# Mixture-of-experts stage: experts ordered by place in group, result rows by expert number, first rows summed during the last experts

## The chip, the core and the metric

One core of one Trainium2 chip runs the program. The metric is device time in microseconds (us) of one execution; the kernel before takes 1620.63 us, the median of three runs.

## What is computed

One layer of a streaming encoder on 1024 tokens of width 1024, in float32: a normalised input, one combined projection, two kinds of attention (8 heads and 4 heads), gates and an output projection. Then comes the stage that the change touches: each token picks one of 4 groups and in it the best 2 of 8 experts, each a gated two-layer network of width 512.

```python
h = rms_norm(x, g_moe)
# group: argmax of h @ w_group; experts: the best 2 of the group's 8
yb = (silu(xb @ w1[e]) * (xb @ w3[e])) @ w2[e]      # for the tokens of expert e
x = x + sum over the token's two experts of weight * yb
out = rms_norm(x, g_final)
```

## The kernel before

**Routing.** While the output projection runs, `route_tile` (L735) finds for 128 tokens at a time the two experts `ix[0]` (higher score) and `ix[1]`, and writes a record into `rec`: token number (plus 1024 for the second choice) and weight. Matmuls with one-hot matrices spread the records into a table of 96 places by 32 experts. From it `slots` (L833) takes `gi` (which rows of the normalised input an expert gathers), `yi` (which row of the result buffer `ys` in DRAM each of its rows is scattered to: row t for the first choice of token t, row 1024 + t for the second) and `wt` (the weights).

**Experts.** `stage_moe` (L1050) goes through the 32 experts in turns e = 0 to 31, in the order of their numbers. PE's order is written out by hand, that of the other engines comes from a scheduler. In turn e PE runs: the 24 matmuls of w3 of this expert (`expert_up`, L971: per slice of 128 inputs one each with the high part, the low part and the high part again, L979 to L981); the 24 of w1 of the next expert, with the transposes of this expert's product `mg` (L998) before the last two slices; the transposes of a gathered input (L967); the 24 matmuls of w2 (`expert_down`, L1011 to L1013). After w3, DVE multiplies silu(w1 part) with the w3 part (`mg`, L990). The result `my` is scaled on ACT (L1018) and scattered to `ys` by POOL (L1022).

**Weights.** Each weight matrix comes in two loads of 1 MB (`expert_piece`, L930, 6 per expert), issued by SP one turn ahead into a ring of 11 slots (`mraw`), with at most three in flight. `expert_split` (L943) splits each into high and low parts: per load two copies on ACT (`mhi`, L45) and two subtractions on DVE (`mlo`, L46), 128x1024 each. A slot is free when its second subtraction is done.

**Tail.** In turn 31 `final_rows` (L1163) loads the rows of x that aren't in SBUF (tiles 0 to 3; 4 to 7 stay in `fx`) and `final_sums` (L1176) both result rows of every token, 1 MB for each of 8 tiles of 128 tokens; POOL adds the first row (L1184). The last expert's result isn't scattered: matmuls with a one-hot matrix `oh` add it in PSUM, together with the second row, which comes in through a matmul with the identity (L1109 to L1111). DVE adds the PSUM halves to x (L1112). `final_norm` (L1189) squares on ACT (L1192), takes the root on ACT (L1194) and the reciprocal on DVE (L1195), multiplies with the gains on DVE (L1196) and stores the tile (L1197).

```python
ps = self.pab.tile([128, 512], F32, name=f"m{n}", bufs=2 - n)
with self.tc.issue_after(self.last_down.ins):
    nc.tensor.matmul(ps, self.ident, Y[t][:, 1, nn], start=True, stop=False)
nc.tensor.matmul(ps, oh[:, t * 128:(t + 1) * 128], hl[0][:, nn], start=False, stop=False)
nc.tensor.matmul(ps, oh[:, t * 128:(t + 1) * 128], hl[1][:, nn], start=False, stop=True)
nc.vector.tensor_add(XS[t][:, nn], ps, XS[t][:, nn])
```

A branch (`overflow`, L1117) serves experts with over 96 tokens; it isn't entered here.

Of the kernel before, what the change touches and what calls it, by code (L numbers as in the profile page):

```python
# [32 lines left out]
CAP = 96  # L33
N_OVF = 21
# [17 lines left out]
class Block:  # L52
# [10 lines left out]
    def constants(self):  # L63
# [9 lines left out]
        self.eps = c.tile([128, 1], F32, name="eps")  # L73
        nc.vector.memset(self.eps, EPS)
# [626 lines left out]
    def route_setup(self):  # L701
# [20 lines left out]
        for k in range(2):  # L722
            nc.vector.tensor_scalar(self.rec[:, :, k, 0], self.tok2[:, :, k], -PAD_ID, None, op0=OP.add)
# [11 lines left out]
    def route_tile(self, t, lg):  # L735
# [194 lines left out]
    def expert_piece(self, e, i):  # L930
# [4 lines left out]
        src = self.a[("w1", "w3", "w2")[wi]][0, e].rearrange("(p c) n -> p c n", p=128)  # L935
# [66 lines left out]
    def expert_down(self, GT, w, wt, y=None, hl=None):  # L1002
        nc = self.nc
        if y is None:
            y = self.xp.tile([CAP, D], F32, name="my", bufs=1)
        ps = [self.py.tile([CAP, 512], F32, name="mpy") for _ in range(2)]
        for k in range(4):
            hi, lo = w[k // 2][k % 2]
            for n in range(2):
                nn = slice(n * 512, (n + 1) * 512)  # L1010
                nc.tensor.matmul(ps[n], GT[0][:, k], hi[:, nn], start=(k == 0), stop=False)  # L1011
                nc.tensor.matmul(ps[n], GT[0][:, k], lo[:, nn], start=False, stop=False)  # L1012
                self.last_down = nc.tensor.matmul(ps[n], GT[1][:, k], hi[:, nn], start=False, stop=(k == 3))  # L1013
        for n in range(2):
# [3 lines left out]
            nc.scalar.activation(y[:, nn], ps[n], AF.Copy, scale=wt)  # L1018
# [31 lines left out]
    def stage_moe(self, st):  # L1050
# [7 lines left out]
        gi, yi = self.gi, self.yi  # L1058
# [5 lines left out]
        for e in range(2):  # L1064
            self.expert_gather(X[e], gi[:, e:e + 1])
        XT = {e: self.expert_x(X[e]) for e in range(2)}
        self.expert_gather(X[0], gi[:, 2:3])
        up0 = self.expert_up(XT[0], weights(0, [0]))
        for e in range(N_EXP):
            last = e == N_EXP - 1  # L1070
            if e == 31:
                XS = self.final_rows(lambda: self.slot(True), self.fx)
# [4 lines left out]
            else:  # L1077
                Y = self.final_sums(self.slot, XS, False)

# [23 lines left out]

        for t in range(NT):
            for n in range(2):
                nn = slice(n * 512, (n + 1) * 512)
                ps = self.pab.tile([128, 512], F32, name=f"m{n}", bufs=2 - n)
                with self.tc.issue_after(self.last_down.ins):
# [4 lines left out]
            self.final_norm(t, XS[t], Y[t].rearrange("p k d -> p (k d)"))  # L1113
        self.yilast = self.rp.tile([CAP, 1], I32, name="yilast")
        nc.vector.tensor_copy(self.yilast, yi[:, N_EXP - 1:])

    def overflow(self):  # L1117
# [3 lines left out]
        with tc.If(n > 0):  # L1121
# [23 lines left out]
            with ExitStack() as st:  # L1145
# [3 lines left out]
                self.final_gains(self.pool(st, "opg", space=PSUM))  # L1149
                self.final_sums(y, X, True)  # L1150
                for t in range(NT):
                    self.final_norm(t, X[t], y())

    def final_gains(self, psum):

        g = self.gfin
        for n in range(2):
            ps = psum.tile([128, 512], F32, name=f"m{n}", bufs=2 - n)
            self.nc.tensor.matmul(ps, self.ones1[0:1, 0:1].to_broadcast([1, 128]), g[0:1, D + n * 512:D + (n + 1) * 512],
                                  start=True, stop=True)  # L1160
# [103 lines left out]
```

## Time and profile before

| | before |
|---|---|
| three runs | 1620.57, 1620.63, 1621.64 us |
| the profiled execution: time, span | 1615.66, 1613.8 us |
| mean granted clock of TensorE | 0.971 |
| PE busy | 1493.0 us (93%) |
| DVE, ACT, POOL busy | 1048.1, 882.5, 288.8 us |
| DMA, mean | 245 GB/s |

The span runs from the first to the last instruction of the profiled execution. Matmuls overlap their neighbours, so a PE that is busy all the time starts one every 0.23 us although each row shows 0.39. A bracket behind a row is the engine's idle time just before it and what ended it.

### The profile page before, as it was taken

The numbers are of one execution on the slowest core, as the hardware profiler recorded it, in microseconds if no ns is written. First come the engines' busy times: TensorE is split into PE (matmuls) and PEld (weight loads), VectorE is DVE, ScalarE is ACT, GpSimd is POOL, SyncE is SP. The second block draws the span as 40 slices with busy tenths as digits, with TensorE's granted clock in tenths as the row PEclk, the third lists the DMA queues.
The fourth block names the chain that finished last, engine by engine and source line by source line (L and its number), as shares of the span: only waits on it lengthen the run. The fifth ranks groups of instructions, "written<-read, shape, count | busy, mean of one in ns | idle before, by whom it ended". The sixth has DMA issues, their size and how long they took to land.

```text
span 1613.8 us, 21890 instructions
## 1 busy us (share of the span) xinstructions
PE 1493.0 (93%) x7713; PEld 1174.4 (73%) x7713; DVE 1048.1 (65%) x1926; ACT 882.5 (55%) x1327; POOL 288.8 (18%) x278
## 2 busy tenths in 40 slices
PE   6996999999999999996999959999999998999996
PEld 6994777777788888885888846666667666666663
DVE  6112555555555545545657459999999888888966
ACT  5212444444454444433312138878888877777764
POOL 2301122222221321210020131131011111111014
PEclk9998999999999999998999979999999999999998
DMA  8927566666644544349934759999999999999936
GB/s 267 332 96 236 139 179 171 164 161 162 159 134 129 166 151 131 111 148 248 313 112 144 313 202 337 377 354 368 385 376 375 374 344 356 346 350 342 351 133 253
DMA packets 181284, 394.94 MB, mean 245 GB/s; under 512 B 21714, under 2 KB 99538, under 8 KB 156594
## 3 DMA queue, kind: packets, MB, share of 16 engines
q1 hardware_dynamic: 174114, 376.89, 69.3%
q0 software_dynamic: 7056, 16.62, 3.1%
q8 instruction: 61, 1.00, 0.3%
q14 instruction: 53, 0.43, 0.1%
HBM read 324.36 MB, written 77.25 MB: 249 GB/s over the span
## 4 chain that ended last, share of the span: by engine, by line
PE 79%; DVE 8%; DMA 6%; issue 4%; ACT 2%; SPq 1%; POOL 1%; ACTq 0%; DVEq 0%; POOLq 0%
PE pz L305 7%; PE pz L306 7%; PE pz L307 7%; PE m L980 6%; PE m L981 6%; PE m L979 6%; PE mpy L1013 3%; PE mpy L1011 3%; PE mpy L1012 3%; DVE mlo L46 3%; PE po L472 2%; PE pt L386 2%; PE ps L360 2%; PE ps L361 2%; DMA mraw<-in_w_dram 2%
## 5 line engine op out<-in xcount | busy, mean ns | idle before, releaser
L46 DVE TENSOR_TENSOR mlo<-mraw,mhi 128x1024 fp32r<-128x1024 f32 x384 | 450.1, 1219 | 40.5 <-ACT mhi L45 38.7
L45 ACT ACTIVATE mhi<-mraw 128x1024 fp32r<-128x1024 f32 x384 | 391.7, 1056 | 64.3 <-PE m L981 46.6
L980 PE MATMUL m<-mlo,XT 128*96 128x512 f32 x512 | 205.6, 402 | 22.3 <-DVE mlo L46 22.3
L305 PE MATMUL pz<-ht,zhi 128*128 128x512 f32 x512 | 215.6, 421 | 0.0
L979 PE MATMUL m<-mhi,XT 128*96 128x512 f32 x512 | 206.5, 403 | 0.0
L981 PE MATMUL m<-mhi,XT 128*96 128x512 f32 x512 | 205.1, 401 | 0.0
L307 PE MATMUL pz<-ht,zlo 128*128 128x512 f32 x512 | 202.5, 396 | 0.0
L306 PE MATMUL pz<-ht,zhi 128*128 128x512 f32 x512 | 201.3, 393 | 0.0
L369 ACT ACTIVATE te<-te,nm 128x256 f32<-128x256 f32 (+7 forms) x128 | 99.2, 775 | 145.1 <-DVE nm L365 145.1
L980 PEld LDWEIGHTS m<-mlo,XT 128*96 128x96 f32 x512 | 84.3, 165 | 64.8 <-DVE mlo L46 31.0
L365 DVE CUSTOM_DVE_ANT_0 te<-ps,nF 128x512 f32<-128x512 f32 (+3 forms) x128 | 75.0, 588 | 76.8 <-PE ps L361 48.6
L46 DVE TENSOR_TENSOR PT<-pt,PT 128x512 fp32r<-128x512 f32 (+1 forms) x144 | 77.0, 554 | 73.3 <-ACT PT L45 71.4
L277 POOL TENSOR_TENSOR zlo<-zraw,zhi 128x1024 fp32r<-128x1024 f32 x32 | 76.7, 2398 | 209.9 <-ACT zhi L276 208.9
L307 PEld LDWEIGHTS pz<-ht,zlo 128*128 128x128 f32 x512 | 96.7, 189 | 21.9
L45 ACT ACTIVATE PT<-pt 128x512 fp32r<-128x512 f32 (+1 forms) x144 | 66.4, 488 | 84.2 <-PE pt L386 57.6
L981 PEld LDWEIGHTS m<-mhi,XT 128*96 128x96 f32 x512 | 84.1, 164 | 35.4 <-issue 0.5
L979 PEld LDWEIGHTS m<-mhi,XT 128*96 128x96 f32 x512 | 84.3, 165 | 34.4 <-issue 0.6
L305 PEld LDWEIGHTS pz<-ht,zhi 128*128 128x128 f32 x512 | 98.4, 192 | 13.5
L306 PEld LDWEIGHTS pz<-ht,zhi 128*128 128x128 f32 x512 | 97.7, 191 | 13.6
L1013 PE MATMUL mpy<-mhi,GT 128*96 128x512 f32 x256 | 101.7, 397 | 2.8 <-DVE GT L46 2.5
L1011 PE MATMUL mpy<-mhi,GT 128*96 128x512 f32 x256 | 102.3, 400 | 0.6 <-ACT GT L45 0.6
L1012 PE MATMUL mpy<-mlo,GT 128*96 128x512 f32 x256 | 100.4, 392 | 0.0
(263 smaller groups left out, 2797.1 us busy)
## 6 DMA issues: line engine op xcount, KB each, us to landing
mraw<-in_w_dram SPq DMA_DIRECT2D x192, 1024.0 KB, 8.1
zraw<-in_w_in_dram SPq DMA_DIRECT2D x32, 512.0 KB, 4.3
ys<-zero SPq DMA_DIRECT2D x16, 512.0 KB, 4.9
gscr<-sh SPq DMA_DIRECT2D x32, 256.0 KB, 2.0
o<-oscr SPq DMA_DIRECT2D x8, 1024.0 KB, 7.5
g<-gscr SPq DMA_DIRECT2D x32, 256.0 KB, 4.5
mraw<-ys SPq DMA_DIRECT2D x8, 1024.0 KB, 10.9
xt<-in_x_dram SPq DMA_DIRECT2D x8, 512.0 KB, 5.0
```

Of the source, the lines that this page charges most:

```text
L45: nc.scalar.activation(hi, src, AF.Copy)
L46: nc.vector.tensor_tensor(lo, src, f32(hi), op=OP.subtract)
L305: nc.tensor.matmul(ps, hi[:, k], self.hT[0][:, k, tk], start=(k == 0), stop=False)
L306: nc.tensor.matmul(ps, hi[:, k], self.hT[1][:, k, tk], start=False, stop=False)
L307: nc.tensor.matmul(ps, lo[:, k], self.hT[0][:, k, tk], start=False, stop=(k == KC - 1))
L369: nc.scalar.activation(t[:, :n], t[:, :n], AF.Exp, scale=-1.0, bias=nm, accum_out=rs)
L979: nc.tensor.matmul(ps, XT[0][:, k], hi, start=(k == 0), stop=False)
L980: nc.tensor.matmul(ps, XT[0][:, k], lo, start=False, stop=False)
L981: nc.tensor.matmul(ps, XT[1][:, k], hi, start=False, stop=(k == KC - 1))
L1011: nc.tensor.matmul(ps[n], GT[0][:, k], hi[:, nn], start=(k == 0), stop=False)
L1012: nc.tensor.matmul(ps[n], GT[0][:, k], lo[:, nn], start=False, stop=False)
L1013: self.last_down = nc.tensor.matmul(ps[n], GT[1][:, k], hi[:, nn], start=False, stop=(k == 3))
```

## The change

- `ORDER` puts the experts in the order 0, 8, 16, 24, 1, 9, ... 7, 15, 23, 31: first each group's first expert, last each group's last.
- In `route_tile` the two records of a token are numbered by expert number: the smaller of its two experts gets row t, the larger row 1024 + t. The last four turns (28 to 31) serve each group's last expert, which is never the smaller one, so rows 0 to 1023 are whole after turn 27's scatter.
- `final_rows` moves from turn 31 to turn 28, with its three slots (they don't go back to the ring), and loads the gains broadcast to 128 partitions. `final_add` replaces `final_sums`: turns 29 and 30 load and add the first rows of four tiles each, turn 31 loads the second rows; all sums are on DVE. The matmuls with the identity, those that spread the gains, and POOL's sums go.
- `final_norm` takes the root by a power on POOL; odd tiles are scaled by one instruction on DVE, even tiles by a copy on ACT and a product on POOL.

```diff
+ORDER = [g * PER_GRP + l for l in range(PER_GRP) for g in range(N_GRP)]
...
-        for k in range(2):
-            nc.vector.tensor_scalar(self.rec[:, :, k, 0], self.tok2[:, :, k], -PAD_ID, None, op0=OP.add)
+        nc.vector.tensor_scalar(self.tok2, self.tok2, -PAD_ID, None, op0=OP.add)
...
+        sw = p.tile([128, 1], F32, name="sw")
+        nc.vector.tensor_scalar(sw, ix[0], ix[1], float(S), op0=OP.is_lt, op1=OP.mult)
+        nc.vector.tensor_add(self.rec[:, t, 0, 0:1], self.tok2[:, t, 0:1], sw)
+        nc.vector.tensor_sub(self.rec[:, t, 1, 0:1], self.tok2[:, t, 1:2], sw)
...
-            if e == 31:
-                XS = self.final_rows(lambda: self.slot(True), self.fx)
...
-            else:
-                Y = self.final_sums(self.slot, XS, False)
+            if e == N_EXP - 4:
+                XS = self.final_rows(lambda: self.slot(True), self.fx)
+            if N_EXP - 4 < e < N_EXP - 1:
+                h = e - N_EXP + 3
+                self.final_add(self.slot, XS, 0, range(4 * h, 4 * h + 4))
+            if last:
+                Y = self.final_add(self.slot, XS, 1, range(NT))
...
+        junk = self.slot(True)
...
-                ps = self.pab.tile([128, 512], F32, name=f"m{n}", bufs=2 - n)
-                with self.tc.issue_after(self.last_down.ins):
-                    nc.tensor.matmul(ps, self.ident, Y[t][:, 1, nn], start=True, stop=False)
-                nc.tensor.matmul(ps, oh[:, t * 128:(t + 1) * 128], hl[0][:, nn], start=False, stop=False)
-                nc.tensor.matmul(ps, oh[:, t * 128:(t + 1) * 128], hl[1][:, nn], start=False, stop=True)
+                ps = self.pab.tile([128, 512], F32, name="m0", bufs=2)
+                for i in range(2):
+                    nc.tensor.matmul(ps, oh[:, t * 128:(t + 1) * 128], hl[i][:, nn], start=(i == 0), stop=(i == 1))
                 nc.vector.tensor_add(XS[t][:, nn], ps, XS[t][:, nn])
...
+    def final_add(self, tile, X, k, ts):
+
+        nc = self.nc
+        Y = {}
+        for t in ts[::2]:
+            y = tile()
+            nc.sync.dma_start(y.rearrange("p (t d) -> p t d", t=2), self.ys[k * S + t * 128:k * S + (t + 2) * 128].rearrange("(t p) d -> p t d", p=128))
+            for i in range(2):
+                Y[t + i] = y[:, i * D:(i + 1) * D]
+                nc.vector.tensor_add(X[t + i], X[t + i], Y[t + i])
+        return Y
...
+        ss = self.fp.tile([128, 1], F32, name=f"ssf{t % 2}")
+        nc.scalar.activation(junk, x, AF.Square, accum_out=ss)
+        r = self.rstd(self.fp, ss, D, f"rf{t % 2}")
+        if t % 2:
+            nc.vector.scalar_tensor_tensor(y, x, r, self.gfin, op0=OP.mult, op1=OP.mult)
+        else:
+            nc.scalar.activation(x, x, AF.Copy, scale=r)
+            nc.gpsimd.tensor_tensor(y, x, self.gfin, op=OP.mult)
+        self.nc.sync.dma_start(self.a["out"][0, t * 128:(t + 1) * 128], y)
```

**DVE between the products of turns 29 and 30**, before. `mg` is the product of a turn (the first here is turn 30's), `mlo` a subtraction of weights; 14789 is the last load of expert 30's w2, 14949 the first of the next expert's w1.

```order
L46 TENSOR_TENSOR mlo<-mraw_14787,mhi 128x1024 x2
L46 TENSOR_TENSOR mlo<-mraw_14789,mhi 128x1024 x2
L46 TENSOR_TENSOR mlo<-mraw_14949,mhi 128x1024
L990 TENSOR_TENSOR mg<-m_14977,mg 96x128x4
L46 TENSOR_TENSOR mlo<-mraw_14949,mhi 128x1024
```

The same place with the change (14826 is the last load of w2, 14994 the first of the next w1; 14649 and 14652 hold x of tiles 0 to 3, 14828 and 14832 their first rows):

```order
L48 TENSOR_TENSOR mlo<-mraw_14824,mhi 128x1024 x2
L48 TENSOR_TENSOR mlo<-mraw_14826,mhi 128x1024 x2
L1187 TENSOR_TENSOR mraw_14649<-mraw_14649,mraw_14828 128x1024 x2
L994 TENSOR_TENSOR mg<-m_15030,mg 96x128x4
L1187 TENSOR_TENSOR mraw_14652<-mraw_14652,mraw_14832 128x1024 x2
L48 TENSOR_TENSOR mlo<-mraw_14994,mhi 128x1024 x2
L48 TENSOR_TENSOR mlo<-mraw_14996,mhi 128x1024 x2
```

Four sums stand ahead of the first subtraction of the last expert's w1, where before one subtraction stood ahead of the product.

**DVE from the last splits to the tail**, with the change (`GT` is the low part of the transposed product of turn 31, X_9655 and the `mlo` beside it the parts of the last expert's result; L1119 is the sum from PSUM, L1112 before):

```order
L48 TENSOR_TENSOR mlo<-mraw_15004,mhi 128x1024 x2
L1187 TENSOR_TENSOR fx_8979<-fx_8979,mraw_15006 128x1024
L994 TENSOR_TENSOR mg<-m_15196,mg 96x128x4
L1187 TENSOR_TENSOR fx_8981<-fx_8981,mraw_15010 128x1024
L48 TENSOR_TENSOR GT_15241<-mpt,GT_15240 128x384
L51 SCALAR_TENSOR_TENSOR mlo<-mpy,sw,X_9655 96x512
L1187 TENSOR_TENSOR mraw_14649<-mraw_14649,mraw_15156 128x1024 x2
L1187 TENSOR_TENSOR mraw_14652<-mraw_14652,mraw_15160 128x1024 x2
L1119 TENSOR_TENSOR mraw_14649<-m_15281,mraw_14649 128x512
L1187 TENSOR_TENSOR fx_8979<-fx_8979,mraw_15164 128x1024
```

Each `fx` sum shown has a second one behind it. Before, nothing stood between the last splits, `mg` and `GT`, and the tail on DVE began with the sums from PSUM.

**SP**, with the change, from turn 28's loads on (14645 is the last load of expert 29, 14647 the gains, 14994 the first load of the last expert):

```order
L940 DMA mraw_14645<-in_w_dram 128x2048
L1169 DMA mraw_14647<-in_g_final_dram 128x1024
L1175 DMA mraw_14649<-x_7590 128x1024 x2
L940 DMA mraw_14816<-in_w_dram 128x2048
L940 DMA mraw_14826<-in_w_dram 128x2048
L1184 DMA mraw_14828<-ys 128x2x1024
L1184 DMA mraw_14832<-ys 128x2x1024
L940 DMA mraw_14994<-in_w_dram 128x2048
L1184 DMA mraw_15006<-ys 128x2x1024
L1184 DMA mraw_15156<-ys 128x2x1024
```

Of the weight loads only the first and last of an expert are shown. The loads of x and of the first rows now stand between the weight loads; before, all stood behind the last one.

## Rows read from the trace of the kernel before

**Rows 1.** Busy time in stretches of the end: start and end, length, busy us and instructions of PE, PEld, DVE, ACT and POOL, granted clock of TensorE, DMA share, GB/s.

```profile
1503.00:1523.00 20.00, 19.31 (x92) 13.49 (x91) 17.97 (x22) 16.54 (x21) 2.10 (x2) 1.00 0.94 355
1543.00:1562.00 19.00, 18.31 (x82) 12.63 (x81) 15.72 (x15) 14.56 (x18) 1.05 (x1) 1.00 0.17 63
1600.00:1614.00 14.00, 3.90 (x12) 1.75 (x10) 6.92 (x11) 3.50 (x9) 0.00 (x0) 0.80 0.38 152
```

**Rows 2.** The timeline (start, duration) of POOL's last four scatters, the issue of the last weight load and of the first result load by SP, and the same stretch's DMA times to landing (last two rows).

```profile
1521.97 1.45 POOL L1022 DMA_INDIRECT ys<-my,sy  x1 [17.53 <-ACT my L1018]
1543.47 1.05 POOL L1022 DMA_INDIRECT ys<-my,sy  x1 [20.05 <-ACT my L1018]
1562.24 1.20 POOL L1022 DMA_INDIRECT ys<-my,sy  x1 [17.72 <-ACT my L1018]
...
1529.91 0.33 SPq L936 DMA_DIRECT2D mraw<-in_w_dram  x1
1565.92 0.37 SPq L1183 DMA_DIRECT2D mraw<-ys  x1
...
mraw<-in_w_dram SPq DMA_DIRECT2D x13, 1024.0 KB, 5.7
ys<-my,sy POOLq DMA_INDIRECT x2, 7.1
```

**Rows 3.** The timeline of DVE around the products of turns 29 and 30.

```profile
1527.53 3.49 DVE L46 TENSOR_TENSOR mlo<-mraw,mhi 128x1024 fp32r<-128x1024 f32 x3
...
1544.17 3.50 DVE L46 TENSOR_TENSOR mlo<-mraw,mhi 128x1024 fp32r<-128x1024 f32 x3 [0.45 <-ACT mhi L45]
1548.08 1.10 DVE L990 TENSOR_TENSOR mg<-m,mg 96x512 f32<-96x512 f32 x1 [0.41 <-PE m L981]
1549.09 4.62 DVE L46 TENSOR_TENSOR mlo<-mraw,mhi 128x1024 fp32r<-128x1024 f32 x4
```

**Rows 4.** PE at the start of w1's matmuls in turn 30, then in turn 29.

```profile
1547.88 0.40 PE L979 MATMUL m<-mhi,XT 128*96 128x512 f32 x1
1548.11 0.39 PE L980 MATMUL m<-mlo,XT 128*96 128x512 f32 x1
1550.35 0.47 PE L980 MATMUL m<-mlo,XT 128*96 128x512 f32 x1 [0.69 <-DVE mlo L46]
...
1528.80 0.47 PE L980 MATMUL m<-mlo,XT 128*96 128x512 f32 x1 [2.03 <-DVE mlo L46]
```

**Rows 5.** Busy time in stretches, columns as in rows 1.

```profile
1530.00:1533.00 3.00, 3.00 (x9) 1.95 (x8) 3.00 (x3) 1.06 (x1) 0.00 (x0) 0.50 0.84 306
1566.00:1568.20 2.20, 0.55 (x4) 0.37 (x4) 1.02 (x1) 0.49 (x1) 0.00 (x0) 1.00 0.48 110
1568.20:1574.00 5.80, 5.78 (x24) 3.71 (x24) 0.56 (x1) 0.54 (x1) 2.87 (x2) 1.00 1.03 421
1585.00:1588.50 3.50, 0.48 (x3) 0.05 (x1) 3.50 (x4) 0.00 (x0) 3.50 (x2) 0.90 1.03 405
1588.50:1594.00 5.50, 5.49 (x9) 3.06 (x10) 2.60 (x4) 2.89 (x6) 3.88 (x2) 0.50 0.39 156
```

**Rows 6.** The timeline of turn 31 on DVE and PE, from the last splits to the last expert's down matmuls.

```profile
1562.94 2.36 DVE L46 TENSOR_TENSOR mlo<-mraw,mhi 128x1024 fp32r<-128x1024 f32 x2 [0.29 <-ACT mhi L45]
1566.02 1.02 DVE L990 TENSOR_TENSOR mg<-m,mg 96x512 f32<-96x512 f32 x1 [0.71 <-PE m L981]
1568.20 0.56 DVE L46 TENSOR_TENSOR GT<-mpt,GT 128x384 fp32r<-128x384 f32 x1 [1.17 <-ACT GT L45]
...
1568.81 0.47 PE L1013 MATMUL mpy<-mhi,GT 128*96 128x512 f32 x1
1573.72 0.40 PE L1013 MATMUL mpy<-mhi,GT 128*96 128x512 f32 x1
```

**Rows 7.** The timeline of the tail: POOL's last sums, the splits of the last expert's result on DVE, two products with the gains on DVE and a sum from PSUM beside POOL's sums, the last product and the last store.

```profile
1581.10 2.37 POOL L1184 TENSOR_TENSOR fx<-fx,mraw 128x1024 f32<-128x1024 f32 x1 [0.19 <-DMA mraw<-ys]
1583.66 8.72 POOL L1184 TENSOR_TENSOR fx<-fx,mraw 128x1024 f32<-128x1024 f32 x3 [0.19 <-DMA mraw<-ys]
...
1574.17 1.45 DVE L49 SCALAR_TENSOR_TENSOR mlo<-mpy,sw,X 96x512 fp32r<-96x512 f32 x2 [5.41 <-ACT X L48]
1582.67 1.89 DVE L1196 SCALAR_TENSOR_TENSOR mraw<-mraw,rfr,mraw 128x1024 f32<-128x1024 f32 x1
1585.14 2.71 DVE L1196 SCALAR_TENSOR_TENSOR mraw<-mraw,rfr,mraw 128x1024 f32<-128x1024 f32 x1
1587.78 0.68 DVE L1112 TENSOR_TENSOR mraw<-m,mraw 128x512 f32<-128x512 f32 x1
1607.02 1.28 DVE L1196 SCALAR_TENSOR_TENSOR mraw<-fx,rfr,mraw 128x1024 f32<-128x1024 f32 x1
1608.34 0.33 SPq L1197 DMA_DIRECT2D out_dram<-mraw  x1
```

**Rows 8.** Durations by line: instructions, count, ns least/median/most, first and last start.

```profile
L125 DVE TENSOR_SCALAR r2m<-ss x8: 153/154/155, 801.0 to 944.7; 128x1 f32<-128x1 f32 x8
L127 POOL TENSOR_TENSOR r1r<-r1m,mhalf x8: 548/550/1583, 6.4 to 36.9; 128x1 f32<-128x1 f32 x8
L1192 ACT ACTIVATE mraw<-fx x4: 1057/1058/1059, 1596.5 to 1605.3; 128x1024 f32<-128x1024 f32 x4
L1192 ACT ACTIVATION_READ_ACCUMULATOR mraw<-fx x4: 185/186/188, 1597.5 to 1606.3; 128x1 f32 x4
```

More of the change, by code (lines that the diff above doesn't have):

```diff
@@ L1012, in expert_down @@
                 nc.tensor.matmul(ps[n], GT[0][:, k], lo[:, nn], start=False, stop=False)
-                self.last_down = nc.tensor.matmul(ps[n], GT[1][:, k], hi[:, nn], start=False, stop=(k == 3))
+                nc.tensor.matmul(ps[n], GT[1][:, k], hi[:, nn], start=False, stop=(k == 3))
         for n in range(2):
@@ L1057, in stage_moe @@
         self.moe_pools(st, True)
-        gi, yi = self.gi, self.yi
+        gi, yi, wt = [[x[:, o:o + 1] for o in ORDER] for x in (self.gi, self.yi, self.wt)]
         def weights(e, ms):
@@ L1148, in overflow @@
                 X = self.final_rows(y, {})
-                self.final_gains(self.pool(st, "opg", space=PSUM))
-                self.final_sums(y, X, True)
+                self.fp = p
+                for k in range(2):
+                    self.final_add(y, X, k, range(NT))
                 for t in range(NT):
[L1152 to L1160, printed above, removed]
-            self.nc.scalar.activation(g[:, n * 512:(n + 1) * 512], ps, AF.Copy)
+                    o = y()
+                    self.final_norm(t, X[t], o[:, :D], o[:, D:])
     def final_rows(self, tile, X):
         nc = self.nc
-        g = self.gfin = tile()
-        nc.sync.dma_start(g[0:1, D:], self.a["g_final"].rearrange("(o d) -> o d", o=1))
+        self.gfin = tile()[:, :D]
+        nc.sync.dma_start(self.gfin, self.bcast(self.a["g_final"]))
         ts = [t for t in range(NT) if t not in X]
@@ L1174, in final_rows, with final_norm @@
         return X
-    def final_sums(self, tile, X, both):
+    def final_add(self, tile, X, k, ts):
         nc = self.nc
-        Y = []
-        for t in range(NT):
-            y = tile().rearrange("p (k d) -> p k d", k=2)
-            Y.append(y)
-            nc.sync.dma_start(y, self.ys.rearrange("(k t) d -> t k d", k=2)[t * 128:(t + 1) * 128])
-            nc.gpsimd.tensor_tensor(X[t], X[t], y[:, 0], op=OP.add)
-            if both:
-                nc.vector.tensor_add(X[t], X[t], y[:, 1])
+        Y = {}
[5 more added lines that the diff above has]
+                nc.vector.tensor_add(X[t + i], X[t + i], Y[t + i])
         return Y
-    def final_norm(self, t, x, y):
+    def final_norm(self, t, x, junk, y):
         nc = self.nc
-        ss = self.rp.tile([128, 1], F32, name="ssf", bufs=2)
-        nc.scalar.activation(y[:, :D], x, AF.Square, accum_out=ss)
-        r = self.rp.tile([128, 1], F32, name="rfr", bufs=2)
-        nc.scalar.activation(r, ss, AF.Sqrt, scale=1.0 / D, bias=self.eps)
-        nc.vector.reciprocal(r, r)
-        nc.vector.scalar_tensor_tensor(y[:, D:], x, r, self.gfin[:, :D], op0=OP.mult, op1=OP.mult)
-        nc.sync.dma_start(self.a["out"][0, t * 128:(t + 1) * 128], y[:, D:])
+        ss = self.fp.tile([128, 1], F32, name=f"ssf{t % 2}")
[3 more added lines that the diff above has]
+            nc.vector.scalar_tensor_tensor(y, x, r, self.gfin, op0=OP.mult, op1=OP.mult)
+        else:
+            nc.scalar.activation(x, x, AF.Copy, scale=r)
+            nc.gpsimd.tensor_tensor(y, x, self.gfin, op=OP.mult)
+        self.nc.sync.dma_start(self.a["out"][0, t * 128:(t + 1) * 128], y)
     def run(self):
```

31 lines of the change are left out of this document (15 added, 16 removed).

## Prediction

> **What bounds the kernel now.** I read the busy time by stretches first. In the experts' stage PE works 19.31 of 20 us and DVE 17.97, in turns 30 and 31 still 18.31 and 15.72 of 19 [rows 1]: PE sets the pace, DVE has some 2 us to spare in a turn, and DMA falls to a share of 0.17 once the last weights are in. In the last 14 us PE is busy 3.90 and nothing runs through. So I look at two things apart: when the last expert's down matmuls end (last start 1573.72 [rows 6], end about 1574.1; I call it T), and how long the tail is from T to the end.
>
> Next come the waits at the joints of the turns. PE starts w1's matmuls at 1547.88 and stops at 1550.35 for a subtraction on DVE [rows 4]; that one began at 1549.09, behind the product at 1548.08 [rows 3]. DVE's place in its list at the joint, not its load over a turn, is what PE feels. In the tail, DVE's last product starts at 1607.02, 34.2 us after T it ends (1608.30), and from there to the end of the span are 5.5 us for store and closing [rows 7]. The tail is 39.7 us.
>
> All terms below are against this profiled execution: 1615.66 us, span 1613.8. The median of the runs is 1620.63; I add the sum to the median. A measurement of this kernel tells about 0.2%, 3.2 us, from no change.
>
> **Routing: +0.4.** Three small DVE instructions more per tile, 153 ns each by the nearest row [rows 8]. Seven of the eight tiles have them beside the output projection's matmuls; without that cover they would cost 0.45 each. The last tile's stand in DVE's list ahead of the records that the first gather waits for: 0.4 (0 to 0.45). The order of the experts itself, the eps constant and the gathers cost nothing: as many rows and bytes move, in another order.
>
> **Loads: 0.** The same 8 MB of result rows are read, 4 MB of them earlier; new are 0.5 MB for the gains. Three of 11 slots leave the ring at turn 28. A weight load goes out as the slot 11 loads back is free: the last one went at 1529.91 [rows 2], when the second of the splits begun at 1527.53 ended [rows 3]. With 8 slots the last expert's loads go when the same-numbered loads of the expert before are split: the first at 1529.9, the last at 1546.5. They are split from about 1546.5 (first) to 1562.94 (last) [rows 3, 6] and land 5.7 us after issue [rows 2]: 10 us to spare. The first-row loads wait on SP for turn 28's scatter, 1521.97 + 7.1 = 1529.1 [rows 2], and the last expert's weights queue behind them, but those had no slot before 1529.9. The scatter of turn 29 now waits on POOL for these loads; they land by about 1537, it goes at 1543.47. Nothing is late; if landings took 10 us more, a rival below.
>
> **Four sums ahead of the last expert's first split: +4.4.** A sum reads two SBUF tiles of 128x1024 like a subtraction of weights: 3.50/3 to 4.62/4 = 1.16 us in a row [rows 3]. DVE ends w2's last split at 1546.5 (1544.17 and two of three). Then, by the list: two sums to 1548.8, the product (1.0) to 1549.8, two sums to 1552.1, the first split to 1553.3. PE has been ready for it since 1548.11 [rows 4]. Before, PE's eighth matmul ran at 1550.35, which is a start without a stop at 1550.35 - 7 x 0.231 = 1548.73; now the second runs at 1553.35, a start at 1553.12. Difference 4.4. The splits after it come every 1.16 us, six matmuls take 1.39, so no second wait. Lower bound 3.3 (if the first pair of sums were done in DVE's gaps), upper 5.
>
> **The clock after that stop: +2.7.** After the stop of 2.03 us in turn 29 [rows 4] the granted clock is 0.50, the 1.2 GHz level, for 3 us and somewhat more; nine matmuls run in a stretch that holds 13 at full clock [rows 5], which with its edges cost 1.65. After 3.02 idle us of PE in the tail the clock is 0.50 for 5.5 us [rows 5]: 2.75 lost. The new stop is over 5 us, nearest to the second: 2.7 (1.6 to 2.75).
>
> **Four sums in turn 31: +2.7.** The last split ends at 1565.30 [rows 6]; two sums take DVE to 1567.6, so the product starts 1.6 later than 1566.02. Two sums follow it, 2.3, ahead of the low part of GT: it starts at 1570.9 in place of 1568.20, and PE's third down matmul needs it. 2.7 (2 to 3). All this on top of the shift already there.
>
> **The clock after that: +1.6.** Before, PE was idle 1.7 us in two pieces here and kept its clock of 1.00 [rows 5]. Now the first piece alone is 2.5 us; the nearest row is the 2.03 of turn 29, priced 1.65. Bounds 0 and 2.75.
>
> **The tail: +3.0.** Off PE go the 32 identity matmuls and the gains; off POOL eight sums of 2.37; off ACT the roots and a table load. On DVE come eight sums of 1.16 and 8 factors of 0.15 in place of reciprocals; four products of 1.28 leave for ACT (1.06) and POOL (2.37 each, as its sums [rows 7]). POOL gets eight powers of 0.55 [rows 8]. DVE's own work is then 8 x 1.16 + 16 x 0.67 + 4 x 1.28 + 2 x 0.73 + 8 x 0.15 = 27.8 us. What matters is who waits for whom in the lists, so I go through them with these durations, 0.07 us per handover.
>
> A product on DVE beside POOL's sums takes 1.89 and 2.71 in place of 1.28, POOL's three sums 8.72 in place of 7.1, while the sum from PSUM keeps 0.68 [rows 7]. So I let instructions that read two SBUF tiles on both engines exclude each other. This way the list of before gives T to the last product 33.9, against 34.2 in the trace; without exclusion it gives 30.4. The new list gives: first split of the result 0.9, two sums 3.3, second split and two sums 6.5, tile 0's halves 7.8, two sums 10.2, tile 1's first half 11.1, a sum 12.3, then DVE waits for POOL's first product until 14.7; the last half of tile 7 ends at 31.3, its square 32.6, factor and power 33.5, its product 34.8; tile 6 has its copy on ACT behind tile 7's square and its product on POOL until 37.2. So 37.2 against 34.2: +3.0. Bounds: 33.9 without exclusion (-0.3), 38.2 if the matmuls run at the lower clock (+4).
>
> The Trainium skill ("SBUF — State Buffer", section Who interferes with whom) says that a VectorE instruction with two SBUF inputs and a GpSimd instruction that reads SBUF hold a shared port for the whole instruction, and that one with a single SBUF input stays free of it. Rows 7 agree for sums and products. For the powers on POOL, 128x1, no run here shows whether they are held up as well in the tail; by the rule they are, and the tail is the 37.2 above, otherwise about 0.5 less.
>
> **Sum.** 0.4 + 4.4 + 2.7 + 2.7 + 1.6 + 3.0 = 14.8, so 1620.6 + 14.8 = 1635.4; I say 1635.
>
> **Rivals.**
> - **DVE waits, no clock, no exclusion.** The joints cost 4.4 + 2.7, the clock nothing (as at 1566 to 1574 [rows 5]) and the tail -0.3: 7.2 with the routing, 1628. For it: the clock's fall isn't the same after each stop. Chance 0.17.
> - **Faster: the sums are free on DVE.** POOL pays 2.37 for a sum, DVE 1.16; if DVE reached the sums of turns 29 and 30 in its 2 us of spare time per turn [rows 1], T would stay, and the tail would be DVE's own 27.8 plus the last copy and product, about 31 against 34.2: 3.2 less, with the routing 1618; with an earlier end of the last square, 1615. It decides if the joints cost under the tail's gain. Against it: DVE's list is kept in order, and at 1544 to 1549 it has 0.45 and 0.41 of idle time [rows 3]. The Trainium skill ("GPSIMD Engine Reference", section 4.1 Engine selection) puts elementwise sums on VectorE, about twice as fast; the prices agree, and by that rule the tail would gain. Chance 0.10.
> - **Weights late.** If the scatter of turn 28 lands 10 us later than 7.1, SP holds the last expert's loads until about 1540 and its splits come at 1548 to 1551: that is still ahead of the sums' end; only beyond does each us count. With 6 us more: 1641. Chance 0.05.
> - **No change.** Joints of 3 to 5 us, and a tail shorter by as much: 1620. Chance 0.06. That the change doesn't move the sums is excluded by the lists.
>
> **How the numbers follow.** Forecast 0.62, for 1635, own range 1630 to 1640. The range 1625 to 1641 takes in the first rival and the bounds of the terms (low 0 + 3.3 + 0 + 2 + 0 - 0.3 = 5; high 0.45 + 5 + 2.75 + 3 + 2.75 + 4 = 18, of which not all are likely at once); it leaves out the two other cases and the late weights. Slower by over 0.2%: 0.62 + 0.17 + 0.05 = 0.84; within: 0.06; faster: 0.10.
>
> **What would show it.** In the profile after: PE idle some 5 us in front of the last expert's second w1 matmul, ended by DVE's subtraction, and behind it a stretch at clock 0.50; an idle time of over 2 us before GT's transposes and a wait for GT's low part; L1187 rows of about 1.16; T about 12 us later, near 1586; then 37 us to POOL's last product. It is wrong if DVE's sums start earlier than w2's last split, if T moves by less than 4 us, or if the tail after T is shorter than 34 us.

## Result and the profile after

Four runs of the changed kernel take 1629.96 to 1634.97 us, median 1630.44; four of the kernel before beside them 1621.11. The ratio is 1.0064 (95% 1.0045 to 1.0082): slower, by 7 to 13 us. The forecast was 1635, its range 1625 to 1641.

The profiled execution took 1629.96, its span is 1628.1, against 1615.66 and 1613.8 before. Of the 14.3 us between the spans 13.4 lie in the last three stretches of this table. I cut at marks that both traces have: POOL's scatters of turns 29 and 30, and DVE's first split of the last expert's result (`mlo` <- `mpy`), which starts at the end of the last down matmul.

| | before | changed | difference |
|---|---|---|---|
| start to the scatter of turn 29 | 1543.47 | 1544.37 | +0.9 |
| from there to the scatter of turn 30 | 18.77 | 23.90 | +5.1 |
| from there to the first split of the result | 11.93 | 16.49 | +4.6 |
| from there to the end | 39.63 | 43.34 | +3.7 |

DVE of the changed kernel, in order of time (start, duration, line, tiles, count, idle time ahead). L48 are the splits, L1187 the sums, L994 `mg`; [rows 3, 6] hold this piece of before:

```profile
1545.07 2.36 DVE L48 TENSOR_TENSOR mlo<-mraw,mhi 128x1024 fp32r<-128x1024 f32 x2 [0.48 <-ACT mhi L47]
1547.35 2.35 DVE L1187 TENSOR_TENSOR mraw<-mraw,mraw 128x1024 f32<-128x1024 f32 x2
1549.62 1.02 DVE L994 TENSOR_TENSOR mg<-m,mg 96x512 f32<-96x512 f32 x1
1550.56 2.35 DVE L1187 TENSOR_TENSOR mraw<-mraw,mraw 128x1024 f32<-128x1024 f32 x2
1552.83 4.62 DVE L48 TENSOR_TENSOR mlo<-mraw,mhi 128x1024 fp32r<-128x1024 f32 x4
...
1571.26 2.35 DVE L1187 TENSOR_TENSOR fx<-fx,mraw 128x1024 f32<-128x1024 f32 x2
1573.53 1.01 DVE L994 TENSOR_TENSOR mg<-m,mg 96x512 f32<-96x512 f32 x1
1574.45 2.35 DVE L1187 TENSOR_TENSOR fx<-fx,mraw 128x1024 f32<-128x1024 f32 x2
1576.72 0.55 DVE L48 TENSOR_TENSOR GT<-mpt,GT 128x384 fp32r<-128x384 f32 x1
1584.76 0.75 DVE L51 SCALAR_TENSOR_TENSOR mlo<-mpy,sw,X 96x512 fp32r<-96x512 f32 x1 [7.49 <-ACT X L50]
```

No sum has idle time ahead of it: DVE goes without a pause from the splits through the sums to `mg` and on to the last expert's first split. The same view of PE shows three places where DVE kept it idle; the bracket says how long and what ended it. [rows 4] have the first place before. The line behind the `...` is before's wait at the second. At the third PE did not wait for DVE before:

```profile
1554.09 0.74 PE L984 MATMUL m<-mlo,XT 128*96 128x512 f32 x1 [4.92 <-DVE mlo L48]
1574.59 0.56 PE L1002 MATMUL mpt<-ident,mg 96*128 96x96 f32 x4 [1.76 <-DVE mg L994]
1577.32 0.74 PE L1016 MATMUL mpy<-mhi,GT 128*96 128x512 f32 x1 [0.43 <-DVE GT L48]
...
1567.09 0.55 PE L998 MATMUL mpt<-ident,mg 96*128 96x96 f32 x4 [1.11 <-DVE mg L990]
```

PE's 0.69 us ahead of the second w1 matmul has become 4.92. The stretches behind it (length, then busy time and count of PE, PEld, DVE, ACT, POOL, then the granted clock, DMA share and GB/s):

```profile
1548.70:1554.00 5.30, 0.47 (x2) 0.00 (x1) 5.30 (x6) 1.19 (x2) 0.00 (x0) 0.73 0.96 359
1554.00:1560.40 6.40, 6.31 (x22) 4.37 (x23) 5.31 (x6) 2.13 (x3) 0.00 (x0) 0.69 0.78 302
1578.00:1584.90 6.90, 6.83 (x23) 4.32 (x21) 0.14 (x1) 0.84 (x2) 0.00 (x0) 0.72 0.80 330
1600.00:1628.10 28.10, 9.52 (x18) 4.43 (x18) 11.93 (x20) 9.76 (x15) 13.40 (x11) 0.50 0.38 151
```

After each stop part of the next 6 to 7 us runs at the lower level (granted clock 0.69 and 0.72 over these stretches), and the end of the tail, where PE is busy for 9.52 of 28.1 us, stays at it (0.50). POOL in the tail (L127 the power, L1200 the product of an even tile):

```profile
1594.32 3.22 POOL L127 TENSOR_TENSOR rf0r<-rf0m,mhalf 128x1 f32<-128x1 f32 x1 [25.14 <-DVE rf0m L125]
...
1616.81 3.28 POOL L1200 TENSOR_TENSOR mraw<-fx,mraw 128x1024 f32<-128x1024 f32 x1 [0.23 <-ACTq L1130]
```

POOL's last product ends at 1620.09, 35.3 us behind the first split, and the span goes on for 8.0 us, where before 5.5 followed DVE's last product [rows 7]. At the end of its list POOL runs a drain of 5.2 us. The changed kernel, then before (count, ns least/median/most, first and last start):

```profile
L1264 POOLq DRAIN  x3: 46/107/5213, 1622.0 to 1627.8; - x3
L1260 POOLq DRAIN  x3: 46/107/5213, 1594.3 to 1613.5; - x3
```

The long one is the first. Before it started at 1594.3, beside other work; now it starts at 1622.0, behind the last product.

### The profile page after: what moved, and what is told of

It is laid out like the page before. It is cut to its first block, busy times and chain, and to the rows that moved or that the text cites. A ratio compares the mean times of both kernels' runs of the same rounds, so it can differ in the third digit from the quotient of the medians.

```text
span 1628.1 us, 21837 instructions
## 1 busy us (share of the span) xinstructions
PE 1491.4 (92%) x7677; PEld 1171.6 (72%) x7677; DVE 1060.3 (65%) x1960; ACT 882.9 (54%) x1320; POOL 286.4 (18%) x282
## 5 line engine op out<-in xcount | busy, mean ns | idle before, releaser
L48 DVE TENSOR_TENSOR mlo<-mraw,mhi 128x1024 fp32r<-128x1024 f32 x384 | 450.1, 1220 | 43.1 <-ACT mhi L47 41.6
L984 PEld LDWEIGHTS m<-mlo,XT 128*96 128x96 f32 x512 | 84.8, 166 | 69.4 <-DVE mlo L48 35.3
L48 DVE TENSOR_TENSOR PT<-pt,PT 128x512 fp32r<-128x512 f32 (+1 forms) x144 | 77.0, 554 | 72.6 <-ACT PT L47 70.6
L305 PEld LDWEIGHTS pz<-ht,zhi 128*128 128x128 f32 x512 | 98.5, 192 | 14.4 <-ACT zhi L276 0.5
```

The source lines that it names most:

```text
L48: nc.vector.tensor_tensor(lo, src, f32(hi), op=OP.subtract)
L305: nc.tensor.matmul(ps, hi[:, k], self.hT[0][:, k, tk], start=(k == 0), stop=False)
L984: nc.tensor.matmul(ps, XT[0][:, k], lo, start=False, stop=False)
```

## Experiments

The table has the median, the ratio to the kernel before on the same chip, and the last two stretches as above: joints (scatter of turn 29 to first split of the result) and tail (from there to the end). The kernel before has other medians beside other runs: 1621.1 beside the changed kernel, 1617.5 beside e2 to e4, 1618.9 beside e5 to e8, 1620.0 beside e9 and e10. So kernels are compared by their ratios, not by their times.

| | us | ratio (95%) | joints | tail |
|---|---|---|---|---|
| before, first profile | | | 30.7 | 39.6 |
| e1 before again | 1617.61 | | 32.3 | 40.5 |
| changed | 1630.44 | 1.0064 (1.0045 to 1.0082) | 40.4 | 43.3 |
| e2 sums one column | 1622.37 | 1.0033 (1.0020 to 1.0045) | 33.7 | 43.3 |
| e3 sums placed | 1621.67 | 1.0024 (1.0015 to 1.0034) | 33.8 | 41.4 |
| e4 products on DVE | 1627.41 | 1.0056 (1.0041 to 1.0071) | 39.6 | 40.6 |
| e5 split before mg | 1619.02 | 1.0003 (0.9991 to 1.0015) | 32.3 | 41.4 |
| e6 norm without POOL | 1624.26 | 1.0045 (1.0031 to 1.0059) | 39.6 | 36.6 |
| e7 first rows on POOL | 1633.02 | 1.0085 (1.0063 to 1.0108) | 42.7 | 43.2 |
| e8 combined | 1613.73 | 0.9976 (0.9962 to 0.9990) | 30.8 | 33.5 |
| e9 order alone | 1620.01 | 1.0008 (0.9997 to 1.0019) | 30.7 | 42.4 |
| e10 gains by DMA | 1617.08 | 0.9984 (0.9972 to 0.9997) | 30.7 | 39.9 |

**e1, the kernel before once more.** No edit.

> The kernel before, unchanged, profiled a second time. Its profiled execution took 1615.66 us where its runs took about 1621. If that profiled execution was by chance a short one, this one takes about 1621, and the place where its rows come later than in the first trace tells what of the difference between the two profiles (14.3 us of span) is no work of the change. If profiling itself makes this kernel shorter, it is again about 1616.

1617.61 us, and twenty runs beside it take 1615.49 to 1622.06. The kernel's own spread is 6.6 us, and the first profile lay at its low end. Neither reading of the expectation is shown: profiled or not, executions differ this much. One source is in the two traces. In the first, PE's stop of 2.03 us in turn 29 is followed by the lower clock [rows 4, 5] and the stops of 1.11 and 0.58 in turn 31 are not; in this one it is the other way round, after stops of the same length (2.02, 1.11 and 0.58). The second profile's stretches over turns 29 and 31:

```profile
1524.00:1534.00 10.00, 7.97 (x36) 5.30 (x35) 9.49 (x13) 5.61 (x6) 0.48 (x1) 1.00 0.95 360
1567.00:1575.00 8.00, 7.42 (x26) 4.64 (x24) 0.56 (x1) 0.95 (x2) 4.25 (x2) 0.79 0.99 396
```

In the first the one has 0.50 in it, the other 1.00 [rows 5]; the loss of 1.6 us has changed its place. A larger part of the spread lies ahead of the stretches compared here: the scatter of turn 29 stands at 1541.08 in e5 and at 1548.38 in e8, whose code up to there differs by one constant. What makes that difference isn't shown.

**e2, the first-row sums without their work.**

```diff
-                nc.vector.tensor_add(X[t + i], X[t + i], Y[t + i])
+                c = slice(0, 1 if k == 0 else D)
+                nc.vector.tensor_add(X[t + i][:, c], X[t + i][:, c], Y[t + i][:, c])
```

> The changed kernel with the eight sums of the first rows cut to one column of 1024 (first rows are left out of the result but for that column); their loads, the order of the experts, the second rows' sums and the norm stay. Theory (the sums stand ahead of mg, GT and the last expert's w1 on DVE): all that the changed kernel lost up to the last down matmul but about 1 us of routing comes back, 8 to 9.5 us; that matmul starts near 1575 on the first trace's scale, no matmul between 1530 and 1584 takes over 0.5 us for lack of clock, and the time is 1620.5 to 1622.5. Rival (the loads of ys beside the weight loads, or the order of the experts, make the turns longer): under 3 us come back, 1627.5 or more.

Of the 9.7 us lost in the joints 6.7 come back in the trace, less than the theory's 8 to 9.5; by the ratios the kernel is 0.31% faster than the changed one, 5.0 us. The loads and the order of the experts stay, so the rival falls. But 3 us are left, and PE still stops:

```profile
1550.83 0.66 PE L984 MATMUL m<-mlo,XT 128*96 128x512 f32 x1 [2.18 <-DVE mlo L48]
```

The clock falls behind it (0.62 over 1550 to 1554), which the expectation denied. What it waits for is the split that before stood ahead of `mg` and now stands behind it: the list has changed at a place where no sum is. (A pair of the one-column sums still takes 0.22 us.)

**e3, the sums at places of their own.** `final_add` only loads; each sum is tied behind a named DVE instruction, and two slots of the ring change places so that no load waits for a later sum.

```diff
+                self.behind = self.last_mul
+                self.late_add(late, 1)
+                with self.tc.issue_after(self.sum.ins):
+                    GT = self.expert_g(g)
+                self.late_add(late, 3)
+            if e == N_EXP - 2:
+                self.late_add(late, 4)
...
+            self.late_add(late2, 1 if t < NT - 1 else 0)
```

> The changed kernel with all its sums, each tied behind a named instruction on DVE: four first-row sums behind GT's low part of turn 30, one between mg and GT of the last turn, three behind the last GT low part, and the second-row sums one tile ahead of the PSUM sums that need them. Theory (where the sums stand costs, not that they are done on DVE): the last down matmul starts 8 to 9 us earlier than in the changed kernel, and the tail loses up to 2 us or gains 2: 1619 to 1624. Rival (DVE has no room for eight more sums of 1.17 us in these turns, wherever they stand): the wait moves to another split and 1627 or more is left.

DVE does all sixteen sums, and the joints are as short as in e2 without their work: 6.6 us back (0.40% by the ratios). So it is the place of the sums that costs. Four of them now stand behind GT's low part of turn 30, and just there DVE of the changed kernel had 2.28 us of idle time:

```profile
1563.75 4.63 DVE L48 TENSOR_TENSOR mlo<-mraw,mhi 128x1024 fp32r<-128x1024 f32 x4 [2.28 <-ACT mhi L47]
```

The stop at the last expert's second w1 matmul stays, as in e2:

```profile
1549.28 0.47 PE L984 MATMUL m<-mlo,XT 128*96 128x512 f32 x1 [2.03 <-DVE mlo L48]
```

**e4, the products on DVE.**

```diff
-        if t % 2:
+        if True:
             nc.vector.scalar_tensor_tensor(y, x, r, self.gfin, op0=OP.mult, op1=OP.mult)
```

> The changed kernel with all eight last products as one instruction on DVE (1.28 us each) in place of four there and four as a scaling on ACT and a product on POOL (2.38 to 3.28 us). Theory (POOL's last product and, behind it, POOL's own closing, 1.4 and 5.2 us, set the end): POOL's closing goes beside the last store, and the end comes 3 to 5 us earlier, 1625.5 to 1627.5. Rival (DVE bounds the tail, as its 14.3 us busy of the first 15.1 behind the last down matmul suggest): four more products on DVE take back what the closing gives, and the time stays within 1.5 us of 1630.

The tail is 2.7 us shorter, in the trace; the times alone (1.0056 against 1.0064) don't decide between theory and rival. POOL still closes last:

```profile
1616.98 0.55 POOL L127 TENSOR_TENSOR rf1r<-rf1m,mhalf 128x1 f32<-128x1 f32 x1 [1.53 <-DVE rf1m L125]
```

This power ends at 1617.53, DVE's last product at 1618.84, the span at 1626.0: 8.5 behind POOL, 7.2 behind DVE.

**e5, e3 with `mg` behind the split.**

```diff
+                w = weights(e, [2])
+                w1 = None if last else weights(e + 1, [0])
+                with self.tc.issue_after(self.half[-1 if last else -4].ins):
+                    g = self.expert_gated(up0, b)
```

> e3_sums_placed with one more tie on DVE: mg of turn 30 stands behind both halves of the last expert's first w1 piece, where it stood in front of them in the changed kernel, in e2 and in e3 (in the kernel before, one half stood ahead of it). In e2 and e3 PE still waited 2.18 and 2.03 us for that split against 0.69 before. Theory (the scheduler's list, not the loads, makes that split late): PE's wait ahead of the last expert's second w1 matmul falls under 1 us, no fall of the clock behind it, and the time is 1.3 us (the wait alone) to 3 us under e3's: 1618.5 to 1620.5 where e3 had 1621.7. Rival (the ys loads bring that w1 piece late): the wait stays near 2 us and the time within 0.7 us of e3's.

PE no longer stops there, its clock is 1.00 over 1546 to 1566, and by the two ratios, whose intervals just touch, the time is 0.21% under e3's. SP issues the last expert's weight loads from 7.94 us behind the scatter of turn 28, as in e3, so the list made that split late, not the ys loads. What is left in the joints, 1.6 us, is a lower clock behind stops of 1.42 and 0.58 in turn 31:

```profile
1566.00:1570.00 4.00, 4.00 (x12) 2.55 (x13) 3.81 (x4) 0.00 (x0) 0.00 (x0) 0.65 0.30 85
```

In e8, with the same list up to there and stops of 1.43 and 0.58, the clock is 1.00 in that place (1573 to 1577) and the joints take 30.8.

**e6, the norm of before.** e4's products, with the root by ACT and a reciprocal by DVE.

```diff
-        r = self.rstd(self.fp, ss, D, f"rf{t % 2}")
+        nc.scalar.activation(r, ss, AF.Sqrt, scale=1.0 / D, bias=self.eps)
+        nc.vector.reciprocal(r, r)
```

> The changed kernel with the final norm of the kernel before on ACT and DVE (square root with its table on ACT, reciprocal and one product on DVE for all eight tiles), so that POOL does nothing behind the last scatter. Theory (the power of the last tile on POOL, and the 8 us that POOL's own closing takes behind it, set the end of e4, 8.5 us behind that power's end; and the first power, held 3.2 us by two DVE sums, held DVE up too): POOL's closing is long over, the end comes about 5.5 us behind the last product, and the time is 2 to 4 us under e4's, 1623.5 to 1625.5. Rival (DVE's 25 us of sums and products bound the tail whatever POOL does): within 1 us of e4's 1627.4.

The tail is 4.0 us shorter than e4's, in the trace. By the ratios, 1.0045 against 1.0056, the kernel is 1.8 us faster, with intervals that overlap, so the times alone don't exclude the rival. DVE's last product now ends 6.0 us before the end of the span, 1622.3, and POOL's long drain starts at 1574.8:

```profile
1615.07 1.28 DVE L1200 SCALAR_TENSOR_TENSOR mraw<-fx,rf1r,mraw 128x1024 f32<-128x1024 f32 x1
...
L1264 POOLq DRAIN  x3: 46/107/5213, 1574.8 to 1622.1; - x3
```

Of the 4.0 us 2.8 lie ahead of DVE's last product, which waits for no power any more, and 1.2 behind it, where POOL closed. So POOL's powers and what it does behind them were on the path, and DVE's work was not the only bound.

**e7, the first-row sums on POOL.**

```diff
-                nc.vector.tensor_add(X[t + i], X[t + i], Y[t + i])
+                (nc.vector if k else nc.gpsimd).tensor_tensor(X[t + i], X[t + i], Y[t + i], op=OP.add)
```

> The changed kernel with the eight first-row sums on POOL (2.37 us each in the trace) in place of DVE (1.17 us), all else as there. POOL is busy for 1 us of a turn. Theory (POOL and DVE do not work on two SBUF inputs at once, as the power's 3.22 us beside DVE's sums showed): DVE's splits of turns 30 and 31, busy for 80 to 90 per cent of them, give up as much as POOL takes, 9.5 us in each turn; some of it falls in DVE's idle time, so the last down matmul is 3 to 9 us later than in e2: 1625 to 1631. Rival (they run side by side): the last down matmul starts as in e2, and the time is 1621 to 1623.5. In both, a scatter queued behind these sums on POOL may start later.

1633.02 us, 2 us past the theory's end, and no better than the changed kernel (1.0085 against 1.0064, the intervals overlap). POOL's sums, then splits on DVE: three single ones that fall beside sums, and a row of three that doesn't (at 1545.70):

```profile
1531.48 13.21 POOL L1187 TENSOR_TENSOR mraw<-mraw,mraw 128x1024 f32<-128x1024 f32 x4 [7.99 <-DMA mraw<-ys]
...
1561.01 12.41 POOL L1187 TENSOR_TENSOR fx<-fx,mraw 128x1024 f32<-128x1024 f32 x4 [14.45 <-DMA mraw<-ys]
```

```profile
1542.35 3.43 DVE L48 TENSOR_TENSOR mlo<-mraw,mhi 128x1024 fp32r<-128x1024 f32 x1
1545.70 3.48 DVE L48 TENSOR_TENSOR mlo<-mraw,mhi 128x1024 fp32r<-128x1024 f32 x3
...
1564.44 3.43 DVE L48 TENSOR_TENSOR mlo<-mraw,mhi 128x1024 fp32r<-128x1024 f32 x1
1567.79 3.43 DVE L48 TENSOR_TENSOR mlo<-mraw,mhi 128x1024 fp32r<-128x1024 f32 x1
```

A sum on POOL takes 3.1 to 3.3 us on average in place of 2.37. Such a split takes 3.43 in place of 1.16 (3.48 for the row of three), which is nearly its own time and that of a sum, 1.16 + 2.37 = 3.53: both pay, and each waits for about as long as the other works. The scatter of turn 29 stood behind these sums on POOL and went out 1.3 us late, so the joints of 42.7, which are counted from it, are 44.0 on the scale of the others. PE stops 4.09 us at the first joint and 6.10 for `mg` of turn 31.

**e8, a version from these.** e5's list and e6's norm; the second rows come through an identity matmul again, as before.

```diff
-            self.late_add(late2, 1 if t < NT - 1 else 0)
...
+                nc.tensor.matmul(ps, self.ident, late2[t][1][:, nn], start=True, stop=False)
```

> e5_split_before_mg with e6's norm, and the second rows no longer summed on DVE: as in the kernel before, an identity matmul brings them into the PSUM sum on TensorE. Theory (the tail of the kernel before, less its 2 us for the gains, its collisions of POOL's first-row sums with DVE's products, 0.6 and 1.4 us, its 3 us stop of PE with a lower clock behind it, and with half the bytes of ys to wait for): from the last down matmul to the end 32 to 36 us where the kernel before took 39.7, and 1611 to 1616 in all, faster than the kernel before by 0.1 to 0.4 per cent. Rival (DVE's PSUM sums and products bound the tail just as they did, and the first rows' sums cost in turns 30 and 31 what they save there): 1617 or more.

Faster than both kernels: 0.10 to 0.38% under the kernel before. The joints take no longer than there, and the tail is 6.1 us shorter than in before's first profile (the two spans are only 1.2 us apart, since this execution reached the scatter of turn 29 4.9 us later; e5, with nearly the same code up to there, reached it 2.4 us earlier than before). Here is the tail of e8, and behind it the first stretch at the same distance from the first split (2.87 us) in e5, which has the second-row sums on DVE:

```profile
1582.00:1600.00 18.00, 17.03 (x51) 9.39 (x50) 14.60 (x23) 9.84 (x19) 0.00 (x0) 1.00 0.57 232
1600.00:1612.60 12.60, 3.07 (x10) 1.51 (x8) 6.25 (x10) 2.90 (x7) 0.00 (x0) 0.71 0.41 169
```

```profile
1576.27:1594.27 18.00, 10.75 (x20) 5.54 (x20) 14.83 (x22) 7.83 (x12) 7.11 (x6) 0.53 0.40 165
```

PE, which now has the second rows too, runs nearly through in e8 and its clock stays at 1.00; in e5 it stops between the tiles and the clock is 0.53. DVE has no sums of two tiles beside its products, and POOL nothing. Three things differ from before's tail here: the first-row sums are gone from POOL, the gains come by DMA, and half the result rows are left to load. Their shares of the 6.1 us weren't measured one by one, but for the gains (e10).

**e9, the order and the routing alone**, on the kernel before.

```diff
+        gi, yi, wt = [[x[:, o:o + 1] for o in ORDER] for x in (self.gi, self.yi, self.wt)]
...
+        nc.vector.tensor_scalar(sw, ix[0], ix[1], float(S), op0=OP.is_lt, op1=OP.mult)
```

> The kernel before with the new order of the experts and the routing for it (three small DVE instructions a tile, sw and its two uses) alone; sums, loads and norm are those of before. Theory (this part costs 0.4 us at most, as forecast): 1619 to 1620 where the kernel before takes 1618.9, no difference that shows. Rival (the order itself costs, since weights and rows of the turns come in another order): 2 us or more.

No difference that shows: 0.08%; the interval reaches from -0.5 to +3 us, so the rival's 2 us is not quite excluded by the times. The profiled joints are those of before. The tail of 42.4 has the instructions of before, two of its products at 2.78 and 2.70 us beside POOL's sums. So a tail of these instructions takes 39.6, 40.5 and 42.4 in three profiles.

**e10, the gains by one broadcast DMA**, on the kernel before.

```diff
-            self.final_gains(self.pab)
...
-        nc.sync.dma_start(g[0:1, D:], self.a["g_final"].rearrange("(o d) -> o d", o=1))
+        nc.sync.dma_start(g[:, :D], self.bcast(self.a["g_final"]))
```

> The kernel before with the final gains fetched broadcast to all partitions by one DMA, as in the changed kernel, in place of two one-row matmuls and two copies; the rest is before's. It tells how much of e8's 5 us needs the early first rows at all. Theory (the tail of before is held by the first-row sums on POOL and by the ys loads of 8 MB, the four matmuls of 1.98 us start it late by that much at most): 0 to 2 us under the kernel before. Rival (the head start of 2 us brings PE to its stop sooner and keeps its clock up, so that e8's whole gain is from here): 4 us or more under it.

0.5 to 4.5 us faster by the times, which decides neither for the theory's 0 to 2 nor for the rival's 4 or more. The profiled tail, 39.9, isn't shorter than before's: PE starts the tiles' matmuls 2 us sooner and then stops twice; both stops begin while POOL's sums still run (to 1595.60):

```profile
1588.40 1.12 PE L1107 MATMUL m<-mraw,ident 128*128 128x512 f32 x2 [2.53 <-DVE mraw L1110]
...
1597.34 2.05 PE L1107 MATMUL m<-mraw,ident 128*128 128x512 f32 x2 [3.38 <-DVE fx L1110]
```

In the traces, then, e8's tail of 33.5 isn't from here. By the times the two can't be told apart (0.9984 and 0.9976, with intervals that overlap), so how much of e8's gain this part would give alone stays open.

## Why the prediction was right, and where it was off

T is the end of the last down matmul, as in the prediction. The scatter of turn 30 waits for copies on ACT, so PE's own rows size the terms better than the marks of the table. In the changed kernel: the first matmul of the last expert's w1, the first of w2 in turn 30, and the first and last of w2 in turn 31. Behind the `...`: before's first matmuls of w2 in these turns ([rows 4, 6] have its first of w1 and its last of w2).

```profile
1548.77 0.40 PE L983 MATMUL m<-mhi,XT 128*96 128x512 f32 x1
1561.57 0.39 PE L1014 MATMUL mpy<-mhi,GT 128*96 128x512 f32 x1
1575.73 0.74 PE L1014 MATMUL mpy<-mhi,GT 128*96 128x512 f32 x1 [0.58 <-ACT GT L47]
1584.31 0.40 PE L1016 MATMUL mpy<-mhi,GT 128*96 128x512 f32 x1
...
1554.71 0.40 PE L1011 MATMUL mpy<-mhi,GT 128*96 128x512 f32 x1
1568.22 0.48 PE L1011 MATMUL mpy<-mhi,GT 128*96 128x512 f32 x1 [0.58 <-ACT GT L45]
```

| term | forecast | measured in this pair |
|---|---|---|
| up to the first w1 matmul of the last expert | 0.4 | 0.9 |
| stop for the first split | 4.4 | 4.2 |
| clock after it | 2.7 | 1.7 |
| waits in turn 31 | 2.7 | 1.1 |
| clock in turn 31 | 1.6 | 2.7 |
| tail | 3.0 | 3.7 |

The prediction names the right places and the right causes there, the sums ahead of `mg`, GT and the last expert's first split on DVE, the lower clock behind the stops, and a longer tail. That its sum, 14.8, comes so near the 14.3 between the two profiles is in part luck: three of its terms are off by 1 us or more, and the errors cancel.

- **Routing, +0.4; loads, 0: not contradicted.** e9 shows no difference, but its interval can't resolve 0.4, and the 0.9 of this pair is small against the spread of the part ahead of it (1541.1 to 1548.4 for the scatter of turn 29). PE's stops in the joints are ended by DVE, and one of 0.58 by ACT as before, none by a DMA. SP issued the first-row loads at 1528.78 and the last expert's from 1530.83, against 1529.1 and 1529.9 forecast.
- **Sums ahead of the last expert's first split, +4.4: right in size, short in cause.** The stop is 4.92 against 0.69, 4.2 more. e2 keeps a stop of 2.18 with the sums' work gone, and e3 one of 2.03 with no sum there: 1.3 to 1.5 of the 4.2 come from the split that went behind `mg` (the sum of the forecast had `mg` in that chain, but put all of it on the sums), and e5 removes it by order alone. The rest is the four sums.
- **The clock after it, +2.7: too much.** From the first w1 matmul to the first of w2 are 12.80 us against 6.83 before, 5.97 more; less the 4.2 of the stop that is 1.7. The lower level lasts to 1557.62, about 3.5 us, as after the 2.03 of turn 29 [rows 5] and not as after the 3.02 of the tail that I took as nearest.
- **Turn 31, +2.7 and +1.6: nearly right in sum, wrong in its parts.** 3.7 against 4.3. PE's waits give 1.76 + 0.43 against 1.11 before, 1.1 more, and not the 2.7 of the forecast; the wait ahead of GT's transposes stayed under the 2 us that were to be a sign of it. The clock gives more: the last w2 takes 8.58 from its first matmul to its last, against 5.50, of which 0.43 is the wait; matmuls take 0.63 up to 1581.28. T came 10.6 us later, not 12.
- **The tail, +3.0: 3.7 in this pair, by another route.** From T to POOL's last product are 35.4, not 37.2 (T is 1584.7), 1.2 more than before's 34.2. The 8.0 us behind POOL's last instruction, where I had left before's 5.5, add 2.5 and are the step that was missing; before, POOL was done with its sums at 1592.38 and its drain lay beside other work. One error of 1.8 hid another of 2.5. The lower bound of -0.3 was no bound: it set a list without exclusion, 33.9, against a trace that has it; without it on both sides it is 33.9 against 30.4.
- **Exclusion of DVE and POOL on two SBUF inputs: held.** e7's rows show both engines slowed, each by about the other's time. For the powers, which I left open, the trace has the answer: 3.22 us beside two DVE sums, 0.55 otherwise. That agrees with the Trainium skill ("SBUF — State Buffer", section Who interferes with whom), by which a VectorE instruction with two SBUF inputs contends with a GpSimd instruction that reads SBUF.
- **The rivals.** "Sums are free on DVE" fell: no sum found idle time. e3 shows what it would have needed, another place in the list. The price that the Trainium skill ("GPSIMD Engine Reference", section 4.1 Engine selection) gives for such sums, about twice as much on GpSimd, holds, 2.37 against 1.16, and says nothing on the list. "DVE waits, no clock, no exclusion" had 1628 us, which is nearer to the 1630.4 than the forecast; only the rows decide against it, since the clock fell behind both stops and the exclusion held.
- **The total, 1635 against 1630.4.** The sum fits the two profiles, but the times are 9.3 us apart, 7 to 13. The profile that the sum was made on was one of before's shortest executions (1615.66, e1's runs 1615.5 to 1622.1), and I added the sum to the median. The other profiles of the same lists lie closer together: joints of 39.6 to 40.4 (changed, e4, e6) against 30.7 to 32.3 (before, e1, e9, e10), tails of 43.2 to 43.3 (changed, e2, e7) against 39.6 to 42.4 (before, e1, e9). Their means differ by 8.8 and 2.4, 11.2 in all, where the forecast has 14.4. So some 3 of the 5 us lie in these stretches, where before takes longer in its other profiles; the rest isn't shown. The range, too, is looser than its sums: the highest is 18, which gives 1638.6 and not 1641, and the lowest takes 0 for a clock term whose own bound is 1.6.

## What to carry to other kernels

An instruction on an engine with spare time is only free at a place in its list where nobody waits for what stands behind it: the same eight sums cost 6.6 us more at one place of DVE's list than at another (changed kernel and e3). Look also at what the scheduler moved besides, here one split past a product. And look at what an engine does after its last instruction before it is given the last work of a kernel; work taken off TensorE in a tail can leave it with stops and the lower clock.

## What the hardware showed that I had not expected

- The span ends 8.0 us behind POOL's last instruction in the changed kernel, e2, e3, e5 and e7 (8.5 in e4), whatever that was, a product or a power of 128x1; 5.2 of it are a drain. Where POOL was done long ago it ends 5.5 to 6.0 behind DVE's last product (before, e1, e6, e8, e9, e10).
- Stops of the same length don't always lower TensorE's clock: after 2.03 us in turn 29 it was 0.50 in the first profile of before and 1.00 in the second, after 1.42 and 0.58 in turn 31 it fell in e5 and not in e8. A fall cost about 1.6 us each time in these four profiles, and 2.7 in turn 31 of the changed kernel.
- Over the 18 us that start 2.87 us behind the first split of the result, the clock is 0.78 to 1.00 in the five profiles that have the 32 identity matmuls in the tail (before, e1, e8, e9, e10) and 0.50 to 0.53 in the seven without them (changed, e2 to e7). No run changed these matmuls alone.
